# Tiles and k-tiles of moving weights from 128-byte to 256-byte boundaries of SBUF, in a two-block transformer kernel

## The chip, the cores and the metric

The kernel runs on one core of a Trainium2 chip. The metric is the device time of one execution in microseconds, the median of several runs. A profile of one execution shows its instructions engine by engine: TensorE (PE for matmuls, PEld for weight loads), VectorE (DVE), ScalarE (ACT), GpSimd (POOL), and SyncE (SP), which issues most of the transfers.

## What is computed

The reference is two transformer blocks in a row over 512 positions of width 1024, in FP32. The first has a gated feed-forward part (FFN), a mixer of three branches and a second FFN. The second has another mixer, an attention to a memory and a third FFN. Cut to what matters here:

```python
x = x + 0.5 * swiglu_ffn(rmsnorm(x, ffn1_norm_g), ffn1_w_in, ffn1_w_out)     # width 2816
q, kv, nsa_g, conv_in, q_mem, merge_g = jnp.split(rmsnorm(x, mix_norm_g) @ w_in, ...)
o_nsa = nsa_attention(...)      # 16 heads of 64: compressed keys, blocks, window of 512
o_conv = short_gated_conv(conv_in, conv_w, conv_b)
o_mem = memory_attention(q_mem, mem, ...)                                  # 256 positions
x = x + (g_nsa * o_nsa + g_conv * o_conv + g_mem * o_mem) @ w_out
x = x + 0.5 * swiglu_ffn(rmsnorm(x, ffn2_norm_g), ffn2_w_in, ffn2_w_out)
# second block
x = x + _mixer_block(_rms(x, norm_mix_w), ...)     # attention in chunks, gated linear attention
x = x + _memory_xattn(...)
x = x + _swiglu(_rms(x, norm_ffn_w), w_ffn_gate, w_ffn_up, w_ffn_down)
return _rms(x, norm_final_w)
```

So nearly all the work is products of a 512 x 1024 activation with weight matrices that are read once.

## The kernel before

Activations are kept transposed, with 128 channels on the partitions and the 512 positions along them, in eight tiles `x` of 2048 bytes to a partition. TensorE multiplies in the type FP32R. To come near FP32, each operand is split into a high and a low part, and each product is three matmuls (`mm3`, L229): high by high, high weights by low activation, low weights by high activation. `matmul(o, l, r)` has `l` as weights, loaded into the array ahead, and `r` as the moving operand, which streams past. In the profile a matmul reads `out<-moving,weights`.

`norm_x` (L389) makes the split activation: a high and a low tile for each of eight `x`, all under the one name `xs`, 16 tiles of 512 columns. `w` (L272) loads a weight unit of 128 x 1024 into `wr`, lets ScalarE round it into `wh`, and VectorE or GpSimd subtract into `wl`. Each name has two or three buffers in a pool. `chunk` (L302) multiplies such a unit with eight k-tiles: 24 matmuls into one PSUM bank, in the order `xs` high with `wh`, `xs` low with `wh`, `xs` high with `wl`, for each k-tile. An FFN (L513) does so for 44 units of `f_ab`, in three groups; after each group the product `uh`, `ul` of the two halves, two names of eight tiles, is the moving operand against units of `f_o`, 21 or 24 matmuls to a bank. In the second mixer `og` (high and low under one name) and `oah`, `oal` (two names) are moving. `qk` is the name of the queries and keys of the first attention; in its compressed branch (`nsa_cmp`, L1010) the queries move against `kph` and `kpl`.

`moving` (L313) is the other way round: the weights `wh`, `wl` move and the activation is loaded. There a unit holds two or four k-tiles of n columns, each beginning on a multiple of `LINEW` elements; n is 280, 456, 384 or 256. In `mem_kv` (L674) the memory's values are made in the same way with 512 columns.

Where a tile lies is set by the pools. `t` (L212) asks for a boundary for all tiles that aren't small:

```python
LINEW = 32
...
    def t(self, pool, shape, dt, tag, bufs=None):
        big = pool is not self.pp and int(np.prod(shape[1:])) >= LINEW
        return pool.tile(shape, dt, tag=tag, name=self.name(tag), bufs=bufs, align_bytes=4 * LINEW if big else None)
```

All buffers of one name in a pool lie behind one another, and the next name begins behind them and some padding. At the start of SBUF lies a scratch, 16384 bytes to a partition, for the descriptors of the transfers that GpSimd issues: the inputs `cols` and `rel`, and the tables `drel`, `dcmp` and `dline` (L496 to L501), which the first attention reads later.

The order of instructions follows the code and a scheduler that hoists them engine by engine; waits are semaphores between engines.

Of the kernel before, what the change touches and what calls it, by code (L numbers as in the profile page):

```python
# [26 lines left out]
OFF = (0, 128, 384, 768)  # L27
OFF2 = (0, 128, 384, 640)

LINEW = 32  # L30

# [167 lines left out]
class _Net:  # L201
# [8 lines left out]
        return f"{s}{self.n}"  # L210

    def t(self, pool, shape, dt, tag, bufs=None):  # L212
        big = pool is not self.pp and int(np.prod(shape[1:])) >= LINEW
        return pool.tile(shape, dt, tag=tag, name=self.name(tag), bufs=bufs, align_bytes=4 * LINEW if big else None)

    def pool(self, name, side=None):
# [55 lines left out]
    def w(self, arr, u, n, split=False, rows=None):  # L272
# [10 lines left out]
        if rows:  # L283
            ku, m = rows
            cut = lambda t: t[:, :ku * (-(-m // LINEW) * LINEW)].rearrange("p (a b) -> p a b", a=ku)[:, :, :m]
            nc.sync.dma_start(cut(raw), self.a[arr][u].rearrange("p (a b) -> p a b", a=ku))
# [26 lines left out]
    def moving(self, arr, u0, n, ku, ah, al, nt, tags, evac):  # L313

        ps = [self.ps(tags[i], (P, n)) if tags else self.psf((P, n)) for i in range(nt)]
        nu = KT // ku
        pitch = -(-n // LINEW) * LINEW
        for u in range(nu):
# [13 lines left out]
    def rsqrt(self, pool, v, shape, tag):  # L332

        y = self.t(pool, shape, F32, tag + "y", 1)
        t = self.t(pool, shape, F32, tag + "t", 1)
        self.ts(t.bitcast(I32), v.bitcast(I32), 1, ALU.logical_shift_right)
        self.ts(y.bitcast(I32), t.bitcast(I32), -1.0, ALU.mult, float(0x5F3759DF), ALU.add)
        for _ in range(3):
            self.mul(t, v, y)
            self.stt(t, t, -0.5, y, ALU.mult, ALU.mult)  # L340
            self.stt(y, t, 1.5, y, ALU.add, ALU.mult)
        return y
# [1445 lines left out]
```

## Time and profile before

| | us |
|---|---|
| median of 3 runs (2503.13 to 2507.59) | 2503.69 |
| the profiled execution | 2503.41 |
| its span, first to last instruction | 2501.3 |
| PE busy, 11566 matmuls | 2433.9 |
| PEld busy, 11566 weight loads | 1997.8 |
| DVE busy | 1434.1 |
| ACT busy | 980.4 |
| POOL busy | 408.6 |

A page gives each engine's busy time and its share of the span, the chain of work that ended last (each piece followed back to what released it), and groups of instructions. Matmuls overlap and their ends are modelled, so that the busy time of PE is not the time that it spends streaming columns. A row of the timeline gives an instruction's start, so differences between starts tell what one costs. A piece of the chain has its start, its length, the engine, the output's name and line, and how many instructions it joins.

### The profile page before, as it was taken

What the parts mean: (1) busy time and instruction counts of PE and PEld (TensorE: products, weight loads), DVE (VectorE), ACT (ScalarE), POOL (GpSimd) and SP (SyncE); (2) the same over time, 40 slices, a digit from 0 to 9 for tenths busy, and PEclk for the clock granted to TensorE, in tenths of its full rate; (3) what the DMA queues carried; (4) which work ended last, traced back from release to release, by engine and by line L of the source; (5) the groups of instructions that cost most, each with busy time, mean ns of one, the idle gap of its engine ahead of it and who ended that gap; (6) DMA issues with size and microseconds to landing.
All of it is one profiled execution on the core that took longest, in us unless ns stands there. A gap on an engine that the chain in (4) does not pass through costs nothing.

```text
span 2501.3 us, 30104 instructions
## 1 busy us (share of the span) xinstructions
PE 2433.9 (97%) x11566; PEld 1997.8 (80%) x11566; DVE 1434.1 (57%) x2594; ACT 980.4 (39%) x1743; POOL 408.6 (16%) x223
## 2 busy tenths in 40 slices
PE   9999999999999999999999999999999999999998
PEld 6888888787777887778888888787788877888887
DVE  7444445865777777775534444658665277534444
ACT  5222234343454444453322223545555346322222
POOL 5000004231222232230000002121212330000000
PEclk9999999999999999999999999999999998999999
DMA  6622225321212121233222323121212241322321
GB/s 197 182 93 94 98 84 171 102 103 49 77 68 76 53 93 61 71 109 111 93 97 89 101 87 102 56 88 55 73 69 73 100 141 70 115 95 93 99 79 48
DMA packets 84051, 232.26 MB, mean 93 GB/s; under 512 B 16305, under 2 KB 25457, under 8 KB 83908
## 3 DMA queue, kind: packets, MB, share of 16 engines
q1 hardware_dynamic: 75460, 224.87, 27.0%
q0 software_dynamic: 8448, 5.48, 0.8%
q8 instruction: 91, 1.49, 0.2%
q14 instruction: 52, 0.43, 0.1%
HBM read 223.85 MB, written 11.64 MB: 94 GB/s over the span
## 4 chain that ended last, share of the span: by engine, by line
PE 48%; DVE 5%; ACT 1%; issue 1%; DVEq 0%; ACTq 0%
PE g L227 25%; PE s L227 11%; PE t L227 11%; PE o L227 1%; PE t L235 1%; DVE q L238 1%; DVE sp L1523 0%; DVE wl L238 0%; DVE xs L250 0%; DVE og L238 0%; DVE ptl L238 0%; ACT wh L256 0%; DVE og L250 0%; DVE stl L238 0%; DVE sq L250 0%
## 5 line engine op out<-in xcount | busy, mean ns | idle before, releaser
L227 PE MATMUL g<-xs,wh 128*128 128x512 f32 x2800 | 899.1, 399 | 0.2
L256 ACT CAST wh<-wr 128x1024 fp32r<-128x1024 f32 (+6 forms) x405 | 410.5, 1015 | 1073.3 <-PE g L227 466.0
L227 PEld LDWEIGHTS g<-xs,wh 128*128 128x128 f32 x2800 | 526.2, 191 | 114.0 <-issue 2.9
L227 PE MATMUL g<-xs,wl 128*128 128x512 f32 x1400 | 560.9, 401 | 1.5 <-DVE wl L238 1.5
L238 POOL TENSOR_TENSOR wl<-wr,wh 128x1024 fp32r<-128x1024 f32 (+6 forms) x134 | 310.6, 2320 | 1455.0 <-ACT wh L256 1418.2
L238 DVE TENSOR_TENSOR wl<-wr,wh 128x1024 fp32r<-128x1024 f32 (+4 forms) x271 | 335.1, 1238 | 76.2 <-ACT wh L256 69.4
L227 PEld LDWEIGHTS g<-xs,wl 128*128 128x128 f32 x1400 | 265.2, 189 | 59.9 <-issue 3.1
L227 PE MATMUL s<-xs,wh 128*128 128x512 f32 x672 | 211.1, 395 | 1.2 <-ACT wh L256 1.2
L227 PE MATMUL t<-xs,wh 128*128 128x512 f32 x672 | 210.1, 394 | 2.0 <-ACT xs L256 1.8
L227 PEld LDWEIGHTS s<-xs,wh 128*128 128x128 f32 x672 | 128.2, 191 | 32.8 <-ACT wh L256 2.7
L227 PEld LDWEIGHTS t<-xs,wh 128*128 128x128 f32 x672 | 127.3, 190 | 31.6 <-ACT xs L256 2.2
L227 PE MATMUL s<-xs,wl 128*128 128x512 f32 x336 | 133.9, 399 | 0.0
L227 PE MATMUL t<-xs,wl 128*128 128x512 f32 x336 | 133.6, 398 | 0.0
L253 ACT ACTIVATE sp<-sp,nm 128x128 f32<-128x128 f32 x192 | 102.0, 532 | 48.3 <-DVE nm L1071 37.1
L238 DVE TENSOR_TENSOR ptl<-t,pth 128x512 fp32r<-128x512 f32 (+1 forms) x128 | 73.0, 604 | 58.1 <-ACT pth L256 57.8
L256 ACT CAST pth<-t 128x512 fp32r<-128x512 f32 (+1 forms) x128 | 61.8, 521 | 100.1 <-PE t L235 99.9
L227 PE MATMUL g<-uh,wh 128*128 128x512 f32 (+1 forms) x242 | 92.8, 384 | 0.0
L227 PE MATMUL g<-uh,wl 128*128 128x512 f32 (+1 forms) x242 | 92.3, 382 | 0.0
L227 PE MATMUL g<-ul,wh 128*128 128x512 f32 (+1 forms) x242 | 91.8, 379 | 0.0
L227 PEld LDWEIGHTS s<-xs,wl 128*128 128x128 f32 x336 | 63.5, 189 | 13.1
L227 PEld LDWEIGHTS t<-xs,wl 128*128 128x128 f32 x336 | 63.2, 188 | 13.2
L250 DVE SCALAR_TENSOR_TENSOR x<-g,x 128x512 f32<-128x512 f32 x35 | 24.2, 692 | 80.9 <-PE g L227 80.7
(468 smaller groups left out, 3934.0 us busy)
## 6 DMA issues: line engine op xcount, KB each, us to landing
wr<-f_ab SPq DMA_DIRECT2D x130, 512.0 KB, 3.5
wr<-f_o SPq DMA_DIRECT2D x48, 448.0 KB, 3.2
wr<-m_f SPq DMA_DIRECT2D x40, 512.0 KB, 3.3
wr<-m_o SPq DMA_DIRECT2D x40, 512.0 KB, 3.4
wr<-f_o SPq DMA_DIRECT2D x24, 512.0 KB, 3.5
wr<-m_q SPq DMA_DIRECT2D x12, 512.0 KB, 3.5
dline<-drel POOLq DMA_DIRECT2D x8, 640.0 KB, 21.3
wr<-m_km SPq DMA_DIRECT2D x8, 512.0 KB, 4.5
```

Of the source, the lines that this page charges most:

```text
L227: self.pm = self.nc.tensor.matmul(o, l, r, start=first, stop=last)
L235: self.nc.tensor.transpose(o, i, self.ident)
L238: (e or self.nc.vector).tensor_tensor(o, x, y, op=op)
L250: self.nc.vector.scalar_tensor_tensor(o, x, s, y, op0=op0, op1=op1)
L253: return self.nc.scalar.activation(o, x, f, **k)
L256: self.nc.scalar.copy(o, x)
```

## The change

`LINEW` becomes 64 elements, 256 bytes. Tiles get that boundary if their elements to a partition are a multiple of 64, no longer if they are 32 or more; k-tiles of moving weights begin on it too, so their pitch goes from 288 to 320 for 280 columns and from 480 to 512 for 456, and stays for the others. The scratch is set to 8192 bytes.

```diff
-LINEW = 32
+LINEW = 64
...
-        big = pool is not self.pp and int(np.prod(shape[1:])) >= LINEW
+        big = pool is not self.pp and int(np.prod(shape[1:])) % LINEW == 0
...
-    nc = bacc.Bacc("TRN2", target_bir_lowering=False, num_devices=1)
+    nc = bacc.Bacc("TRN2", target_bir_lowering=False, num_devices=1, dynamic_dma_scratch_size=8192)
```

On every engine the same instructions stand in the same order before and after. What moves is addresses, and three semaphore waits on ScalarE. In the built programs the tiles that matmuls read begin so many bytes past a multiple of 256:

| tile | role in matmuls | before | after |
|---|---|---|---|
| `xs` | moving in 6216 of 512 columns | 0 | 0 |
| `wh` | weights | 0 | 0 |
| `wl` | weights | 128 | 0 |
| `uh`, `oah` | moving | 128 | 0 |
| `ul`, `oal` | moving | 0 | 0 |
| `og`, `oxh`, `oxl` | moving | 128 | 0 |
| `qk` | moving, weights | 128 | 0 |
| `kph`, `kpl` | weights | 0, 128 | 0, 0 |
| `wh`, `wl` in `mem_kv` and at 384 columns | moving | 0, 128 | 0, 0 |
| second k-tile of `wh`, `wl` at 280 and 456 columns | moving | 128, 0 | 0, 0 |
| `mh`, `ml` in `mem_kv` | weights | 128 | 0 |

Of 10702 matmuls in FP32R, 5554 read both operands from a multiple of 256 bytes before, and 10638 do after; nearly all others after have the narrow row statistics `rsh`, `rsl` as weights.

## Rows read from the trace of the kernel before

**Rows 1.** The page: busy time by engine, and the chain's shares by engine.

```profile
PE 2433.9 (97%) x11566; PEld 1997.8 (80%) x11566; DVE 1434.1 (57%) x2594; ACT 980.4 (39%) x1743; POOL 408.6 (16%) x223
...
PE 48%; DVE 5%; ACT 1%; issue 1%; DVEq 0%; ACTq 0%
```

**Rows 2.** The chain, 1246 to 1282 us: start, length, engine, output, line, count.

```profile
1248.37 5.55 PE s L227 x24
...
1259.43 5.49 PE t L227 x24
```

**Rows 3.** PE in order of time at 1253 us: start, length, engine, line, operands.

```profile
1253.52 0.40 PE L227 MATMUL s<-xs,wl 128*128 128x512 f32 x1
1253.75 0.40 PE L227 MATMUL g<-uh,wh 128*128 128x512 f32 x1
```

**Rows 4.** The chain, 1779 to 1786 us, second mixer, moving `og`.

```profile
1781.22 3.50 PE g L227 x15
```

**Rows 5.** Stretch 1753.9 to 1756.9: busy times by engine, granted clock, DMA.

```profile
1753.90:1756.90 3.00, 3.00 (x9) 2.33 (x8) 2.81 (x10) 2.67 (x8) 0.00 (x0) 0.50 0.51 175
```

**Rows 6.** PE in order of time in that stretch.

```profile
1755.20 0.63 PE L227 MATMUL g<-og,wh 128*128 128x512 f32 x1
1755.63 0.63 PE L227 MATMUL g<-og,wl 128*128 128x512 f32 x1
```

**Rows 7.** PE in order of time, compressed keys, first and ninth of a row.

```profile
647.16 0.39 PE L227 MATMUL s<-qk,kph 128*128 128x512 f32 x1
...
649.02 0.33 PE L227 MATMUL s<-qk,qk 128*128 128x128 f32 x2
```

**Rows 8.** Matmuls by form: operands, shape, count, busy us, mean ns of one.

```profile
L227 PE MATMUL g<-xs,wh 128*128 128x512 f32 x2800 | 899.1, 399 | 0.2
L227 PE MATMUL g<-xs,wl 128*128 128x512 f32 x1400 | 560.9, 401 | 1.5 <-DVE wl L238 1.5
L227 PE MATMUL s<-xs,wh 128*128 128x512 f32 x672 | 211.1, 395 | 1.2 <-ACT wh L256 1.2
L227 PE MATMUL t<-xs,wh 128*128 128x512 f32 x672 | 210.1, 394 | 2.0 <-ACT xs L256 1.8 <-DVE xs L238 0.2
L227 PE MATMUL s<-xs,wl 128*128 128x512 f32 x336 | 133.9, 399 | 0.0
L227 PE MATMUL t<-xs,wl 128*128 128x512 f32 x336 | 133.6, 398 | 0.0
L227 PE MATMUL g<-uh,wh 128*128 128x512 f32 x221 | 87.0, 393 | 0.0
L227 PE MATMUL g<-uh,wl 128*128 128x512 f32 x221 | 86.4, 391 | 0.0
L227 PE MATMUL g<-ul,wh 128*128 128x512 f32 x221 | 85.8, 388 | 0.0
...
L227 PE MATMUL t<-uh,wh 128*128 128x512 f32 x140 | 55.0, 393 | 0.0
...
L227 PE MATMUL s<-uh,wh 128*128 128x512 f32 x139 | 54.7, 393 | 0.0
...
L227 PE MATMUL g<-og,wh 128*128 128x512 f32 x128 | 42.4, 409 | 0.0
```

**Rows 9.** The core's span and mean granted clock.

```profile
core 0: 2501.3 us, clock 0.989
```

**Rows 10.** POOL in order of time: the last `dline` and what follows it.

```profile
74.46 1.07 POOL L496 DMA_DIRECT2D dline<-drel  x1 [9.73 <-DMA dline<-drel]
364.83 2.40 POOL L238 TENSOR_TENSOR wl<-wr,wh 128x1024 fp32r<-128x1024 f32 x1 [289.30 <-ACT wh L256]
```

**Rows 11.** The tile `dline`: its transfers from issue to landing.

```profile
DMA to landing us min/median/max: 2.6/20.6/24.3
```

**Rows 12.** PE in order of time, the memory's values: first and seventh of a row.

```profile
409.96 0.39 PE L227 MATMUL g<-wh,mh 128*128 128x512 f32 x1
...
411.33 0.39 PE L227 MATMUL g<-wh,mh 128*128 128x512 f32 x1
```

## The prediction

> **What bounds the kernel now.** I read the page's busy shares first, then its chain of work, then the matmuls by form, then single stretches of the chain and of the order of time. TensorE is busy for 97% of the span, and the chain that ended last is mostly its matmuls: its named shares add up to 55% of the span, further back it is not followed, and 48 of these points are TensorE's against 5 of VectorE and 1 each of ScalarE and issue [rows 1]. So the time is, above all, the number of matmuls times the time from the start of one to the start of the next; I call that the step. The busy column is no measure of it: one matmul of 512 columns is shown as nearly 400 ns because its pipelined end is modelled. A step is read from pieces of the chain: a piece's length over its count.
>
> A piece of 24 matmuls with `xs` as moving operand takes 5.55 us, which is 231.25 ns a step; 91 such pieces are among the chain's longest [rows 2]. A piece of 24 with `uh` and `ul` takes 5.49 us, 228.8 ns, and there are 14 of these [rows 2]; the stretch of `xs` ends and that of `uh` begins at 1253.75 us [rows 3]. Shape, type, line and count are the same in both. Weights come from the same tiles `wh` and `wl`, in the same places. What differs by the program is where the moving tiles begin: `xs` always on a multiple of 256 bytes (I say on the even half), `uh` 128 bytes past one (the odd half), `ul` on the even half again. With `og`, on the odd half throughout, fifteen take 3.50 us, 233.3 ns [rows 4]. So the step does vary by 4.5 ns with something that goes with the place.
>
> The stretches at the lower clock say of what kind the extra is. At a granted clock of 0.50, that is 1.2 GHz, successive starts are 0.43 us apart [rows 5, 6], and 512 columns at 1.2 GHz are 427 ns. At the upper level they would be 213 ns, and 229 to 233 are seen. So there is an excess of 16 to 20 ns that only the faster clock shows; it is this excess that the place of the operands could change.
>
> **The change part by part.** Order and number of instructions stay as they are. The one part that can matter is the place of the operands: afterwards every moving operand of the FP32R matmuls is on the even half, and so are all weights but the narrow row statistics. Before, the weights `wl` lay on the odd half in every third matmul of `xs`.
>
> What does a step cost when nothing lies on the odd half? No stretch of the trace shows that repeated. I get it by difference. I write (even, odd) for moving on the even and weights on the odd half. A triple of `xs` goes (even, even), (even, even), (even, odd) and round again: one step in which nothing changes, one into and one out of an odd `wl`. In the compressed keys of the attention, `qk` moves on the odd half and the weights alternate, `kph` even and `kpl` odd; there a pair is one change of the weights' half and one back. From 647.16 to 649.02 us eight steps take 1.86 us, so a pair takes 465 ns [rows 7]. If only the relation of the halves counts, these are the same two steps as in `xs`, and the step in which both operands are on one half and stay there is 3 x 231.25 - 465 = 228.75 ns. The same subtraction for `og`, (odd, even), (odd, even), (odd, odd), gives 3 x 233.3 - 465 = 235 ns for the step in which moving and weights are on different halves and stay so. Agreement is cheap and disagreement dear, and after the change all agree. I take 228.75 ns.
>
> The bounds: the cheapest kind of matmul in the `uh` stretch is shown at 388 ns where the mean of its three kinds is 390.7 (393, 388, 391) [rows 8], so no kind is more than 2.7 ns below its stretch; the lower end is 228.8 - 2.7 = 226.1 ns. The upper end is the 235 ns of the dear step. 228.75 lies nearest to the stretch that is at 228.8 already.
>
> The sum, with counts from the forms [rows 8]. Moving `xs`: 2800 + 1400 + 2 x 672 + 2 x 336 = 6216 matmuls, 2.5 ns each, 15.5 us. `og`: 128 with `wh` and, by the program, 64 with `wl` and 48 of the same kind in the second memory attention, 240 x 4.55 = 1.1 us. `uh` and `ul`, 3 x (221 + 140 + 139) = 1500, with, by the program, 3 x 64 of `oah` and `oal` and 3 x 32 of the memory's values, together 1788: 228.8 before, so nothing. The narrower matmuls I set at nothing: some 2,200 of them by the program, half a ns each either way would be 1.1 us. That makes 16.6 us if every matmul were on the path at full clock. The mean granted clock is 0.989 [rows 9], so 2.2% of the span is at half clock, where there is no excess to lose; and of the chain's named share, 55%, some 12% is other engines, most of it in the attention stretches, where a faster matmul only meets the wait earlier. 16.6 x 0.978 x 0.88 = 14.3 us.
>
> Three more edits have one answer, nothing. The k-tiles of the moving weights go from a pitch of 288 to 320 and of 480 to 512 elements: the same bytes are loaded and split, and their second k-tile leaves the odd half; 384 matmuls, counted with the narrow ones. Tiles such as `tm` lose their boundary, but no wide matmul reads them. Three waits of ScalarE are put elsewhere, for transfers and matmuls that ended long before.
>
> The halved scratch is for the transfers that GpSimd issues. Of the eight of `dline`, it waits 9.73 us for one before it issues the last at 74.46 us; its next work is at 364.83 us, after 289.30 us of idle time [rows 10]. If half the scratch made it wait out each of the eight, at 24.3 us, the longest landing in the rows on that tile [rows 11], that is 195 us from 55 us on, done by 250 us. Idle time hides it; without that cover it would put some 175 us more on GpSimd's queue, ahead of its next split of weights.
>
> One rule of the Trainium skill speaks against any effect, and the row stands first: with the same shapes, 5.55 us and 5.49 us for 24 [rows 2], so something beyond the column count decides. The Trainium skill, TensorE: Matmul & The Clock Gate, "Part 2: What happens when you issue a matmul", says that the engine has two independent read ports and that loading the next weights takes no read bandwidth from the running matmul; by that alone the halves of moving and weights could not matter to each other and the sum would be 0. The trace does not show it so for FP32R operands, but a difference between two stretches is not yet a proof that the half is the cause.
>
> **The rivals.** *The alternation is what is cheap (slower).* The two stretches at 228.8 have moving halves that alternate: `uh` odd, `ul` even; and `wh`, `wl` as moving for the memory's values, six steps in 1.37 us, 228.3 ns [rows 12]. By counting disagreements, one in three and two in three, these should cost as much as `xs` or more, and they cost less; that speaks against my price. All three stretches with a constant moving half are dearer: 231.25, 232.5, 233.3. Afterwards all are constant. At their mean, 232.35 ns, `xs` loses 1.1 x 6216 = 6.8 us and the 1788 lose 3.55 ns each, 6.3 us; with 0.2 back on `og`, 12.9 us slower, times 0.978, gives 2516 us. It decides from a step of 230.8 ns on, the mean of the 8244 now. At 235 ns throughout it would be 2537.
>
> *Nothing happens.* The differences come from something that the change leaves, such as the order of high and low parts or the distance between tiles: no step moves, and the time stays at 2503 us. The rule of the Trainium skill's page TensorE: Matmul & The Clock Gate that is told above would give the same. Against it: stretches of one instruction and one shape come out at 228.8, 231.25, 232.5 and 233.3.
>
> *More is gained.* Without the odd half each step falls to the lower end, 226.1 ns: 6216 x 5.15 + 1788 x 2.7 + 240 x 7.2 = 38.6 us, times 0.86, is 33 us, 2470 us. For it: some steps are that short. Against it: the path pays whole stretches, and none of those read is below 228 ns a step.
>
> **How the numbers follow.** Forecast 0.48, slower by alternation 0.22, nothing 0.17, more gained 0.13. The profiled execution took 2503.41 us, 2.1 outside its span, 0.3 under the median of the three runs. 2503.4 - 14.3 = 2489.1; I say 2489. The range goes from 2472, short of the fourth case's centre, to 2519, past the second's; it leaves out most of the fourth and the dear end of the second, under 2 in 10. The forecast's own range is 2482 to 2497. About 0.2%, 5 us, is what a measurement of this kernel can tell from no change. Faster by more: 0.47 of the forecast, the fourth, 0.02 of nothing, 0.62. Slower by more: 0.20 of the second and 0.03 of nothing, 0.23. Within: 0.15.
>
> **What would show it.** In the chain afterwards, pieces of 24 at 5.49 us with `xs` and with `uh` alike, fifteen of `og` at 3.43; TensorE's counts unchanged; half-clock share still near 2%. Pieces at 5.57 for both would mean the alternation; 5.55 and 5.49 unchanged, that the half is not the cause; 5.43, the fourth case. I am wrong if steps that agree are not cheap when they are repeated, which no row here shows.

## The result

| | before | after |
|---|---|---|
| median of four runs, us | 2505.07 (2503.13 to 2507.59) | 2481.72 (2480.74 to 2485.23) |
| ratio, 95% interval | | 0.9909 (0.9892 to 0.9926) |
| profiled execution and its span, us | 2503.41, 2501.3 | 2480.74, 2478.7 |

The change makes the kernel 23.4 us faster by the medians. The sign and the kind of the forecast held; its size, 14.3 us, was too small. The page after, where [rows 1] stand for before: busy time by engine, and the chain's shares.

```profile
PE 2406.0 (97%) x11566; PEld 1990.4 (80%) x11566; DVE 1433.1 (58%) x2594; ACT 980.3 (40%) x1743; POOL 407.7 (16%) x223
...
PE 47%; DVE 5%; ACT 1%; issue 1%; POOL 0%; DVEq 0%; ACTq 0%; POOLq 0%
```

The counts are those of before. TensorE fell by 27.9 us of modelled time and its weight loads by 7.4; the other engines are within 1.1 us of before. The core's span and mean granted clock, for [rows 9]:

```profile
core 0: 2478.7 us, clock 0.989
```

The clock is the same to the third digit, so none of the gain is the clock's. The chain of work around the place of [rows 2] (start, length, engine, output, line, count):

```profile
1235.69 5.44 PE g L227 x24
1241.13 5.44 PE s L227 x24
1246.57 5.44 PE g L227 x24
```

And TensorE's work in order of time where the `xs` end and the `uh` begin, for [rows 3]:

```profile
1246.18 0.39 PE L227 MATMUL s<-xs,wl 128*128 128x512 f32 x1
1246.41 0.39 PE L227 MATMUL g<-uh,wh 128*128 128x512 f32 x1
```

Pieces on either side of 1246.41 us are equally long: 5.44 us for 24, a step of 226.7 ns, where `xs` had 5.55 and `uh` 5.49 [rows 2]. Of the chain's pieces of 24 matmuls, 106 now take 5.44; before, 91 took 5.55 and 14 took 5.49. Fifteen of `og` come to 229.3 ns, with other work around them, against 233.3 [rows 4]:

```profile
1769.33 3.44 PE g L227 x15
```

The matmuls by form (count, busy us, mean ns of one), for four of [rows 8]:

```profile
L227 PE MATMUL g<-xs,wh 128*128 128x512 f32 x2800 | 892.2, 396 | 1.3 <-DVE kcr L238 1.0 <-DVE xs L250 0.2
L227 PE MATMUL g<-xs,wl 128*128 128x512 f32 x1400 | 553.2, 395 | 1.5 <-DVE wl L238 1.5
L227 PE MATMUL g<-uh,wh 128*128 128x512 f32 x221 | 86.1, 390 | 0.0
L227 PE MATMUL g<-ul,wh 128*128 128x512 f32 x221 | 86.0, 389 | 0.0
```

`xs` with `wl` fell from 401 to 395 ns, with `wh` from 399 to 396, `uh` from 393 to 390; `ul`, which lay with `wh` on the even half before, went from 388 to 389. What was dear is gone and what was cheap stayed. GpSimd, for [rows 10], the fourth and the last of the `dline` transfers and what follows:

```profile
75.78 1.07 POOL L496 DMA_DIRECT2D dline<-drel  x1 [14.26 <-issue]
...
99.48 1.07 POOL L496 DMA_DIRECT2D dline<-drel  x1 [2.54 <-issue]
360.89 2.40 POOL L238 TENSOR_TENSOR wl<-wr,wh 128x1024 fp32r<-128x1024 f32 x1 [260.34 <-ACT wh L256]
```

With half the scratch GpSimd waits more often between its issues, as was feared, and issues the last 25 us later; the 260.34 us of idle time behind it hide that.

**Where the 22.6 us of span came from.** I paired the 11566 matmuls of the two traces in their order, which is the same, and took the time from each start to the next. "Wide" is 512 columns FP32R; the third column sums the steps of those that neither trace shows waiting or at half clock (under 245 ns in both, 8103 in all).

| stretch of before, us | wide matmuls | gained in steady steps, us | gained in all, us |
|---|---|---|---|
| 100 to 380, first FFN | 1212 | 4.3 | 4.3 |
| 380 to 1100, projections and attention | 2040 | 5.0 | 0.8 |
| 1100 to 1500, second FFN | 1693 | 6.5 | 6.4 |
| 1500 to 1980, second mixer | 1289 | 3.6 | 2.6 |
| 1980 to 2110 | 389 | 1.3 | 3.1 |
| 2110 to the end, third FFN | 1529 | 5.8 | 5.4 |
| all, with the first 100 us | 8512 | 27.9 | 22.4 |

The ledger adds up to 22.4, since it ends with the last matmul's start. Where wide matmuls stand alone, nearly all of the steps' gain arrives. From 1980 to 2110 us more arrives than that: the granted clock of this stretch was 0.93 before and 0.97 after. With the old pitch (`e4_pitch480`, below), where the wide steps are those of the changed kernel, it was 0.95, and the stretch took 128.0 us rather than 127.1. So a part of these 3.1 us is the clock's.

From 380 to 1100 us, with the attention, 5.0 us of shorter steps leave 0.8, and most of the difference is the clock's too. The same matmuls in the kernel before, in the changed kernel, and in the kernel before with the scratch alone halved (`e2_scratch_only`, below, whose steps are those of before); each row has the stretch, its length, the busy times of PE, PEld, DVE, ACT and POOL, the granted clock and DMA:

```profile
380.21:1100.05 719.84, 690.28 (x3592) 569.72 (x3590) 501.87 (x1090) 322.56 (x657) 201.00 (x99) 0.99 0.25 83
376.10:1095.17 719.07, 688.44 (x3592) 571.50 (x3591) 501.08 (x1090) 322.48 (x657) 200.58 (x99) 0.98 0.25 83
381.26:1104.35 723.09, 693.40 (x3592) 571.62 (x3591) 501.72 (x1090) 321.98 (x657) 200.93 (x99) 0.98 0.26 82
```

Steps that one of the first two traces has at the half clock account for 3.2 of the 4.3 us that did not arrive. TensorE's idle time before these matmuls rose from 29.6 to 30.6 us, so longer waits took back 1.0. Against the third row, at the same clock, the changed kernel gains 4.0 of the 5.0 us.

Over the kernel 0.80 of the sum arrived, at the same mean clock. TensorE's idle time before matmuls is 57.9 to 59.9 us in the four whole kernels where steps of `xs` are dear, and 61.4 to 63.4 in the three where `xs` is cheap. So some 3 of the 5.5 us that are missing are longer waits, as they come where the engine reaches the same wait earlier; the rest is within what one execution differs from the next (the span of `e2_scratch_only` is 3.0 us longer than that of before, with the same steps).

### The profile page after: what moved, and what is told of

It is laid out like the page before. It is cut to its first block, busy times and chain, and to the rows that moved or that the text cites. A ratio compares the mean times of both kernels' runs of the same rounds, so it can differ in the third digit from the quotient of the medians.

```text
span 2478.7 us, 30104 instructions
## 1 busy us (share of the span) xinstructions
PE 2406.0 (97%) x11566; PEld 1990.4 (80%) x11566; DVE 1433.1 (58%) x2594; ACT 980.3 (40%) x1743; POOL 407.7 (16%) x223
## 4 chain that ended last, share of the span: by engine, by line
PE 47%; DVE 5%; ACT 1%; issue 1%; POOL 0%; DVEq 0%; ACTq 0%; POOLq 0%
PE g L227 24%; PE s L227 11%; PE t L227 10%; PE o L227 1%; PE t L235 1%; DVE q L238 0%; DVE sp L1523 0%; DVE wl L238 0%; DVE xs L250 0%; DVE og L238 0%; DVE ptl L238 0%; ACT wh L256 0%; DVE og L250 0%; DVE x L238 0%; DVE stl L238 0%
## 5 line engine op out<-in xcount | busy, mean ns | idle before, releaser
L227 PE MATMUL g<-xs,wl 128*128 128x512 f32 x1400 | 553.2, 395 | 1.5 <-DVE wl L238 1.5
L227 PE MATMUL t<-xs,wh 128*128 128x512 f32 x672 | 208.8, 392 | 2.1 <-ACT xs L256 1.9
L238 POOL TENSOR_TENSOR y<-y,rmb 128x512 f32<-128x512 f32 x2 | 3.6, 1786 | 402.8 <-ACT rmb L256 402.8
```

Source lines behind the costliest of these rows:

```text
L227: self.pm = self.nc.tensor.matmul(o, l, r, start=first, stop=last)
L238: (e or self.nc.vector).tensor_tensor(o, x, y, op=op)
```

## The experiments

### Is it the weights' half?

One tile family of the changed kernel is put back 128 bytes past a multiple of 256.

```
-        l = self.t(wp, [P, wc], F32R, "wl", nb)
+        if wp.name not in self.padded:
+            self.padded.add(wp.name)
+            wp.tile([P, 40], F32, tag="pad", name="pad" + wp.name, bufs=1)
+        l = wp.tile([P, wc], F32R, tag="wl", name=self.name("wl"), bufs=nb, align_bytes=128)
```

> The changed kernel with one thing undone: the tiles of the weights' low part (wl) begin 128 bytes past a multiple of 256; everything else stays on multiples of 256, scratch halved. Place of the weights against the moving operand (my theory): a third of the wide matmuls is dear again, pieces of 24 with xs take 5.55 us as before the change (231.25 ns a step) and those with uh too, which were at 5.49 before; 8244 steps x 4.55 ns x 0.85 = 32 us more than the changed kernel: about 2513 us, above the kernel before. Rival, the moving side (the gain came from uh, og, qk and the k-tiles leaving the odd half) or something else than place: xs and uh stay at 5.44, the time within 5 us of the changed kernel's 2481.7.

Measured: 2505.76 us, ratio to the kernel before 1.0006 (0.9996 to 1.0017). The whole gain is gone. The chain of this kernel at the place of [rows 2]:

```profile
1248.28 5.55 PE s L228 x24
1253.83 5.55 PE g L228 x24
```

All pieces are at 5.55, those of `uh` too, as expected; 107 of them are. The rival that the gain came from the moving side alone falls. The time was expected at 2513; the loss is 24.0 us rather than 32, because the price of a step (3.9 ns in the mean over the steady wide steps, by the pairing, for the 4.55 that I took) and the share that arrives (24.0 of 31.2 us, 0.77 for 0.85) were both set too high.

### Is that edit alone enough?

The kernel before, with `wl` on a multiple of 256 and every other tile that TensorE reads left on its half.

```
-        h = self.t(wp, [P, wc], F32R, "wh", nb)
-        l = self.t(wp, [P, wc], F32R, "wl", nb)
+        h = wp.tile([P, wc], F32R, tag="wh", name=self.name("wh"), bufs=nb, align_bytes=256)
+        l = wp.tile([P, wc], F32R, tag="wl", name=self.name("wl"), bufs=nb, align_bytes=256)
```

> The kernel before with one family of tiles moved: wl, the low part of the weights, begins on a multiple of 256 bytes instead of 128 past one. Every other tile that TensorE reads keeps its half (xs even, uh and og odd, k-tiles packed), the scratch is not halved. Distance theory: the 6216 matmuls of xs are all at distance 0, 226.7 instead of 231.1 ns, pieces of 24 at 5.44 us; uh and ul then are odd and even by turns over even weights, 230.1 by the map's patmalt (5.52 us) instead of 228.8; og stays at 233. 6216 x 4.4 less 1500 x 1.3 is 25 us, times 0.81 (what of the sum of steps came through in the other runs) 20: about 2484 us. Rival, that the whole set of halves is needed: xs does not fall to 5.44 and less than 12 us is gained.

Measured: 2486.25 us, ratio 0.9934 (0.9919 to 0.9949), 15.7 us under the kernel before as it was measured beside it (2501.90). Its chain where `xs` end (at 1247.40 us) and `uh` begin:

```profile
1242.12 5.44 PE s L227 x24
1247.56 5.49 PE g L227 x24
```

`xs` is at 5.44 with nothing but `wl` moved; `uh`, odd and even by turns over weights that are all even, stays at 5.49. So `wl` carries two thirds or more of the gain (15.7 of 23.4 us by the medians, 18.3 of 22.4 by the traces), and the rest needs the moving tiles on the same place.

Two parts of the expectation missed. Some 20 us were expected: `xs` fell by 3.7 ns in the mean of its steady steps, not by 4.4. And `uh` was expected at 5.52. By the pairing its three kinds of steps (`uh` with `wh`, `ul` with `wh`, `uh` with `wl`) take 232.3, 226.0 and 228.4 ns, as before (232.5, 226.3, 228.5): it makes no difference to them whether `wl` is on the half of `uh`, as before, or on the other, as here. In an order that mixes places the price is not settled pair by pair.

### Which places agree?

Stretches of one matmul shape, apart from the kernel. The edit is the kernel's whole body:

```
for a in range(8):
    for b in range(8):
        stretch("m" + "abcdefgh"[a] + "w" + "abcdefgh"[b], 512, [(8 * a, 8 * b)])   # moving, weights: elements past a multiple of 256 bytes
```

> This kernel computes nothing of the reference (its output is zeros): it is 64 stretches of 24 matmuls, all of 512 columns FP32R with the same 128x128 weights' size, that differ only in the address of the operands. Stretch m<a>w<b> has its moving operand a x 32 bytes past a multiple of 256 bytes and its weights b x 32 bytes past one (a, b from 0 to 7, written a to h). Relation of the halves (my theory): the step depends on both together. 226.7 ns (24 in 5.44 us), as in the changed kernel, where both begin in the same 128 bytes, and dearer, 229 to 235 ns (5.50 to 5.64 us), where they don't; so mawa = mewe = 5.44, mawe = mewa dearer. Weights' place alone: every row w<e..h> is dearer whatever the moving operand's, so mewe is as dear as mawe. Moving place alone: mewa as dear as mewe, mawe cheap. Place of no weight (the gain came from something else than addresses): all 64 at one value, within 0.02 us.

The chain of the first row, moving operand on a multiple of 256 bytes, weights 0 to 224 bytes past one:

```profile
15.82 5.45 PE mawa L34 x24
21.27 5.59 PE mawb L34 x24
...
38.07 5.60 PE mawe L34 x24
...
49.27 5.51 PE mawg L34 x24
54.78 5.59 PE mawh L34 x24
```

And pieces of other rows, moving operand 32, 128 and 224 bytes past a multiple:

```profile
65.98 5.48 PE mbwb L34 x24
...
194.05 5.60 PE mewa L34 x24
...
205.25 5.51 PE mewc L34 x24
...
216.35 5.45 PE mewe L34 x24
...
366.78 5.44 PE mhwh L34 x24
```

In these rows, each of which repeats one pair of places, the price goes by the distance from the moving operand to the weights, modulo 256 bytes, and not by where either lies: `mewe` is as cheap as `mawa`, `mewa` as dear as `mawe`. I mean distance in this sense from here on. By the starts, steady steps (a row without its first three and last two) are 226.7 ns at distance 0 in seven of the eight rows (227.7 in `mbwb`), 228.7 to 229.1 at 192 (the weights 64 bytes before the moving operand), and 232.5 to 234.5 at the six others. My theory had two halves; in truth 32 bytes off is as dear as 128.

### What the shapes and the patterns of before cost

Stretches of other widths, weight columns and types, and the orders of halves in which the kernel before placed its operands.

```
pats = dict(xs=[(0,0),(0,0),(0,32)], uh=[(32,0),(0,0),(32,32)], kph=[(32,0),(32,32)], malt=[(0,0),(32,0)], ...)   # moving, weights
stretch("bfeven", 512, [(0, 0)], wide=False)
stretch("bfodd", 512, [(0, 64)], wide=False)
```

> Computes nothing of the reference (output zeros): stretches of 24 matmuls with the moving operand on a multiple of 256 bytes and the weights on one (even) or 128 bytes past one (odd), for 512, 480, 456, 448, 384, 320, 280, 256, 192 and 128 columns (na to nj), for fewer weight columns (ca: 512 columns with 64, cb: 512 with 32, cc: 256 with 64, cd: 256 with 32), and in bf16 (bfeven, bfodd); and stretches of 48 matmuls that repeat the placements of before: patxs (moving even, weights even, even, odd), patuh, patmem, patog, patkph, patmalt (weights even, moving even and odd by turns), patfar, patfarw, patall (all even, 2 KB further on). Collision of the two streams by place: naeven 5.44 us for 24 and naodd dearer; the excess over columns / 2.4 GHz is 13.3 ns for each width in the even stretches, as the changed kernel shows for 512, 384 and 256; patxs 11.10 for 48 (231.25 ns), patuh 10.98, patkph 11.16, patog 11.20 as before the change; patfar, patfarw and patall 10.88. If fewer weight columns are loaded there is less to collide: caodd nearer to caeven. Place of no weight: even = odd everywhere and all patterns alike at 10.88. Alternation is what is cheap: patmalt, patuh below patfar and naeven.

```profile
127.99 11.10 PE patxs L34 x48
139.09 11.02 PE patuh L34 x48
172.29 11.15 PE patkph L34 x48
183.43 11.04 PE patmalt L34 x48
216.27 10.88 PE patall L34 x48
227.15 5.20 PE bfeven L34 x24
232.35 5.18 PE bfodd L34 x24
```

Places alone bring back the steps of before: `patxs` 231.1 ns and `patuh` 229.5 by the starts for [rows 2]'s 231.25 and 228.8. `patmalt`, in which the moving half alternates, is dearer (230.1) than `patall`, in which nothing does (226.7): alternation is not what is cheap. But the distances of single pairs don't give these figures: with 226.7 and 233.1 ns for distance 0 and 128, one dear pair in three makes 228.8 for `patxs`, and two in three 231.0 for `patuh`. Why such orders cost what they do stays open; the runs show only that the order of places brings it about.

In bf16 the half makes no difference and a step takes 215.8 ns by the starts. The load of the weights takes 188 ns for FP32R and 97 for bf16 in these traces, beside the running matmul. Two things were not as expected. With 64 weight columns the two halves do come close for 512 columns (230.0 and 229.3 ns), but by the even one getting dearer; 256 columns get cheaper by it (113.4 for 119.6). And the even rows do not all leave the same excess over the columns at 2.4 GHz: it is 13.3 ns for 512 columns, 16.6 for 480 and 18.5 for 456.

### Does each width have its own cheapest distance?

```
for a, n in (("a", 512), ("b", 480), ("c", 456), ("d", 384), ("e", 280), ("f", 256)):
    for w in range(8):
        stretch("n" + a + "w" + "abcdefgh"[w], n, [(0, 8 * w)])
```

> Computes nothing of the reference (output zeros): stretches of 24 matmuls with the moving operand on a multiple of 256 bytes and the weights w x 32 bytes past one (wa to wh), for 512 (na), 480 (nb), 456 (nc), 384 (nd), 280 (ne) and 256 columns (nf), for 512 columns with 64 weight columns (hw), and 512 columns with weights 8, 16, 24, 176, 184, 200 and 208 bytes past a multiple (finea to fineg). The map of offsets gave for 512 columns 226.7 ns at a distance of 0, 228.7 at 192 bytes (64 bytes before the moving operand) and 233 to 234.5 at the other multiples of 32. If the cheap distance belongs to the length of the stream (the loads meet the stream always at the same place of it), each width has its own cheapest distance: 456 and 256 columns, which lost 4 and 2 ns a step by the change, are cheapest at another distance than 0, by 2 to 5 ns a step; and fine stretches lie between their neighbours. If distance 0 is cheapest as such, it is so at each width, and the loss of the narrow ones has another cause. No distance makes 512 columns cheaper than 226.7.

Steady steps in ns by the starts, with the distance in bytes:

| columns | 0 | 32 | 64 | 96 | 128 | 160 | 192 | 224 |
|---|---|---|---|---|---|---|---|---|
| 512 | 226.7 | 233.2 | 233.2 | 234.4 | 233.1 | 233.3 | 228.7 | 233.5 |
| 480 | 216.9 | 213.3 | 216.3 | 217.9 | 219.9 | 219.8 | 218.2 | 220.1 |
| 456 | 208.8 | 206.6 | 206.7 | 206.6 | 206.6 | 205.5 | 207.5 | 208.4 |
| 384 | 173.3 | 173.3 | 174.5 | 173.3 | 175.9 | 176.6 | 173.3 | 176.7 |
| 256 | 119.7 | 118.3 | 117.7 | 117.5 | 118.8 | 119.9 | 117.7 | 117.8 |
| 512, 64 weight columns | 230.5 | 231.5 | 232.6 | 226.6 | 229.1 | 230.1 | 228.3 | 231.1 |

In the chain, 480 columns show it best:

```profile
60.85 5.19 PE nbwa L34 x24
66.05 5.12 PE nbwb L34 x24
```

Yes: 480 columns are cheapest at 32 bytes, 512 columns with 64 weight columns at 96, 256 columns at 64 to 96 and at 192 to 224. Distance 0 is right for 512 and 384 columns, and the worst or nearly so for 456 and 256. These two lost by the change (by the pairing 204.7 to 208.8 and 118.0 to 119.2 ns); the 204.7 of the mixed places before is below every constant distance. Seven finer distances for 512 columns, multiples of 8 bytes, gave 230.0 to 233.4, and not smoothly (230.7, 233.4 and 230.0 at 8, 16 and 24 bytes). For 512 columns none was cheaper than distance 0. The 981 steady steps of 256 columns at their best distance, 117.5 ns, would save 1.7 ns each, 1.6 us in all by this estimate; no run tried it. One execution gave each figure; the 512 columns with 64 weight columns at distance 0 have 230.0 in one run and 230.5 in the other, so a few tenths mean nothing.

### Does a constant disagreement cost what the map says?

Both weight tiles 128 bytes off, moving tiles as in the changed kernel.

```
-        h = self.t(wp, [P, wc], F32R, "wh", nb)
-        l = self.t(wp, [P, wc], F32R, "wl", nb)
+        wp.tile([P, 72 if wp.name == "f1" else 40], F32, tag="pad", ...)     # once for each pool
+        h = wp.tile([P, wc], F32R, tag="wh", name=self.name("wh"), bufs=nb, align_bytes=128)
+        wp.tile([P, 64 if wp.name == "f1" else 32], F32, tag="padb", ...)    # once for each pool
+        l = wp.tile([P, wc], F32R, tag="wl", name=self.name("wl"), bufs=nb, align_bytes=128)
```

> The changed kernel with both weight tiles, wh and wl, 128 bytes past a multiple of 256, all moving tiles still on one: nothing alternates any more, all weights are on the half that the moving operand is not on. Distance theory, by the map: every wide step costs 233.2 instead of 226.7 ns; 8103 steady steps x 6.5 ns x 0.87 = 46 us more than the changed kernel, about 2527 us, and pieces of 24 with xs and with uh at 5.59 us. Rival, that one constant half per operand is what is cheap (no alternation), wherever it lies: 2482 us and pieces at 5.44. Rival, that what costs in the kernel with only wl moved is the change of half between wh and wl: under 2505.

Measured: 2513.92 us, ratio to the kernel before 1.0041 (1.0030 to 1.0053): slower than before, and 32 us slower than the changed kernel.

```profile
1239.32 5.57 PE s L228 x24
1244.89 5.59 PE t L228 x24
```

Nothing alternates here and nearly every piece is dear, 5.57 to 5.60. This excludes, inside the kernel, that a constant place for each operand is what is cheap, wherever it lies. My 2527 missed: a steady wide step has 232.55 ns in the mean, 5.05 more than the changed kernel's 227.5 (the map's 6.5 are for a row that repeats one pair of tiles), and 8116 x 5.05 = 41 us, of which 32 arrived, 0.79.

### The two other edits

The scratch alone, in the kernel before:

```
-    nc = bacc.Bacc("TRN2", target_bir_lowering=False, num_devices=1)
+    nc = bacc.Bacc("TRN2", target_bir_lowering=False, num_devices=1, dynamic_dma_scratch_size=8192)
```

> The kernel before with only the scratch of the descriptors halved (8192 bytes); tiles keep their halves, all addresses move down by 8192. My theory: nothing, 2505 us within 5; pieces of 24 with xs 5.55, uh 5.49. Rival, that the gain came from the scratch or the shift of all addresses: 2482 us and pieces at 5.44.

Measured: 2504.36 us, ratio 0.9997 (0.9987 to 1.0006); pieces of `xs` at 5.55. It does nothing, and neither does moving all addresses by a multiple of 256.

The pitch of the moving weights alone put back, in the changed kernel:

```
-        pitch = -(-n // LINEW) * LINEW
+        pitch = -(-n // 32) * 32
```

> The changed kernel with the k-tiles of the moving weights packed as before (pitch 288 and 480 elements instead of 320 and 512, so that the second k-tile begins 128 bytes past a multiple of 256). 192 matmuls of 456 columns had got dearer by the change, 204.7 to 208.8 ns; their second k-tile would come back to a mixed distance: 0.8 us less at most, 280 columns unchanged (128 ns). Distance theory: 2481 us, within 2 of the changed kernel. Rival, that this edit carried part of the gain (these are moving operands that left the odd half): 3 us or more is lost.

Measured: 2481.67 us (2480.41 to 2482.70), where the changed kernel has 2481.72. By the pairing, steps of 456 columns are back at 204.7 ns. The edit carries none of the gain; the 0.8 us that it may cost can't be seen in the time.

### Do the loads collide in the partition?

```
rows("low" + ..., 512, [(0, 0, 8 * w)])                    # partition, moving, weights
rows("alt" + ..., 512, [(0, 0, 8 * w), (64, 0, 8 * w)])
```

> Computes nothing of the reference (output zeros): stretches of 48 matmuls of 512 columns. full and fullodd: all 128 partitions, weights at distance 0 and 128. lowa to lowh: only partitions 0 to 63 are read, weights at a distance of 0 to 224 bytes. alta to alth: by turns partitions 0 to 63 and 64 to 127, so that the weights loaded next lie in other partitions than the moving operand that is read meanwhile. paira and paire: two and two. If weights' load and moving stream collide in the partition that both read: low as full, 226.7 at distance 0 and 233 at 128, and alt without the excess at every distance, 216 ns or less (as bf16, 215.8), pair between. If what they share is not the partition's memory but something common to all partitions: alt as low, distance for distance. (Row halves may also run beside each other; then alt is far below 213 ns and says nothing.)

```profile
15.59 10.89 PE full L34 x48
26.48 11.16 PE fullodd L34 x48
37.63 11.11 PE lowa L45 x48
82.38 11.16 PE lowe L45 x48
...
126.93 5.21 PE alta L45 x44
```

Inconclusive. The two halves of the partitions ran beside each other, 44 matmuls in 5.21 us, the case in which the run was expected to say nothing. Half the partitions cost the same as all: `lowe` 11.16 as `fullodd`; `lowa` holds a dearer start in its 11.11, its steady steps are 226.9 ns. What it is in the chip that makes the distance matter, and whether anything collides, stays open.

### Why the row that I subtracted hardly moved

In the changed kernel all operands of the compressed keys are at distance 0, and yet the seven steps between its eight starts take 1.613 us, 230.4 ns each; before, the same seven took 231.9 [rows 7]. (The 231.4 of the expectation below comes from starts rounded to 0.01 us.)

```profile
642.58 0.39 PE L227 MATMUL s<-qk,kph 128*128 128x512 f32 x1
...
644.20 0.39 PE L227 MATMUL s<-qk,kpl 128*128 128x512 f32 x1
```

These eight stand right behind matmuls of 280 columns, among busy engines. The last run tells these two apart.

```
st2("prea", [(280, 0, 0)] * 24)
st2("quiet", [(512, 0, 0)] * 48)
st2("preb", [(280, 0, 0)] * 24)
st2("short", [(512, 0, 0)] * 8)
...                                   # VectorE and ScalarE copy tiles under dve, act, both, bothodd
```

> Computes nothing of the reference (output zeros). Question: why the rows of eight with qk over kph and kpl stay at 231.4 ns a step in the changed kernel, where all operands are at distance 0, while xs goes at 226.7. quiet, short, shortodd: 48, 8 and 8 matmuls of 512 columns right behind 24 of 280 columns (as kph and kpl stand), at distance 0, 0 and 128 bytes; quietb: 24 at distance 0 behind 256 columns; quietodd: 48 at distance 128. dve, act, both: 48 at distance 0 while VectorE, ScalarE or both copy 512 KB tiles in SBUF; bothodd the same at distance 128. Entry theory: behind narrow matmuls the loads of weights are out of step with the stream and a row of eight is over before they are in it: short is at 229 to 232 ns, quiet starts so and goes down to 226.7 later. Neighbours theory: it is the other engines' traffic in SBUF: quiet and short at 226.7 from the start, dve, act or both above 228. If all are at 226.7, neither is the cause and it stays open. The distance's price of 5.7 ns is expected beside busy engines too (bothodd less both).

```profile
32.35 1.83 PE short L47 x8
...
37.25 1.87 PE shortodd L47 x8
...
47.46 11.16 PE quietodd L47 x48
58.62 10.88 PE dve L47 x48
69.50 10.88 PE act L47 x48
80.38 10.89 PE both L47 x48
91.27 11.17 PE bothodd L47 x48
```

Eight behind narrow ones take 1.83 us, 229 ns a step, and the long row behind the same narrow ones opens with the same steps (226, 236, 228, 233, 230 ns) before it goes on at 226.7. Busy neighbours cost nothing: 10.88 for 48 under either engine's copies. So the entry theory accounts for most of it: a row of eight is mostly entry. How dear an entry is varies: another such row of the changed kernel, behind 280 columns too (from 888.80 us), has 228.6 ns a step, and the row of `e3_both_odd` at the place of the first, with these operands at distance 0 as well, has 227.0. At 128 bytes the price is the same with busy neighbours (11.17) and without (11.16).

## Why the prediction was right in sign and too small

- *What bounds the kernel, and that the place matters*: right. The excess over the columns at full clock is the operands' affair: places alone make 226.7 to 234.5 of it for FP32R.
- *The aligned step, 228.75 ns*: this is the term that was off. It measured 226.7, close to the lower bound, 226.1, that the cheapest form of [rows 8] had given. The subtraction took a pair of `kph`, `kpl` [rows 7] for one change of half and one back. The map's long `patkph` (232.1 ns by the starts) shows that it goes wrong in long rows too: 3 x 231.1 - 2 x 232.1 = 229.1, not 226.7, so steps in a pattern do not add up pair by pair. And the kernel's own row is of eight behind narrow matmuls, dear by its entry: it came out at 230.4 when its halves agreed.
- *Agreement of halves as the cause*: right for this change and wrong as a rule. Operands on the same half but 32 bytes apart are as dear as on different halves (`mawb` 233.2, `mawe` 233.1). The change puts both at distance 0, which for 512 columns is the cheapest; the theory did not know that no other place in the half would do, and in that the forecast had luck.
- *6216 of `xs` at 2.5 ns*: mis-sized for that reason. 4.6 ns in quiet stretches, 3.9 in the mean of the steady steps by the pairing.
- *1788 of `uh`, `oah` and the memory at nothing*: mis-sized. `uh` had its own dear steps (232.5 ns for `uh` with `wh`) beside the cheap ones; their pieces fell by 2.1 ns a step.
- *Narrow ones at nothing, 1.1 us either way*: they lost about 1.5 us on balance in steps without a wait, by distances that are worse at 256 and 456 columns.
- *The factor, 0.978 x 0.88 = 0.86*: a little high or about right; of the sum of steady steps 0.80 arrived here by the traces and 0.84 by the medians, and 0.70 to 0.79 by the medians in the runs with other places. The reason given, waits met earlier, fits some 3 us of longer waits in the kernel; in the attention it took 1.0 us, and the clock took the most.
- *Scratch and pitch at nothing*: right, each by its own run.
- *Rivals*: that alternation is cheap is excluded by the result, in which nothing alternates and the pieces are at 5.44, and by `patmalt`; no effect, by the result. The fourth case, 226.1 ns, had the price nearly right (226.7). Its 33 us were too much because it gave all 6216 of `xs` the gain of the quiet stretches, 5.15 ns, where 3.9 came in the mean. The time fell between it and the forecast.
- The rule of two independent read ports, in the Trainium skill, TensorE: Matmul & The Clock Gate, "Part 2: What happens when you issue a matmul", would have made distance irrelevant. For bf16 the stretches agree (215.8 ns at both halves); for FP32R the map does not (226.7 to 234.5). Whether it is the reading of the weights that costs the time, no run here shows. The same page of the Trainium skill, "Wait — 56ns, not 53.3ns?", gives 215.7 ns for 512 columns; only the bf16 rows here show it.

## What to carry to other kernels

Where FP32R matmuls of 512 columns with 128 weight columns run back to back, put weights and moving operand at the same place modulo 256 bytes; for other shapes measure the distance, since each has its own. Take the price of a step from a long, quiet row of one shape, never from a short row behind another shape, and do not subtract rows that mix patterns. Of a gain in steps, expect nearly all of it where matmuls stand alone. Where a stretch gives back less, compare its granted clock in both traces before putting it down to waits.

## What the hardware showed that was not expected

- In a row that repeats one pair of FP32R operands, the price repeats with their distance modulo 256 bytes, with a second cheap place at 192 for 512 columns (228.7 ns), and it belongs to the width of the matmul: 480 columns have 213.3 ns at 32 bytes and 216.9 at 0.
- At each of 512, 480 and 384 columns the best distance leaves the same excess over the columns at 2.4 GHz, 13.3 ns (226.7, 213.3 and 173.3 ns), where bf16 leaves 2.5 (215.8).
- A row settles: behind 280 columns some five steps of 226 to 236 ns come before 226.7.
